# A decoder layer on one core: the second norm's chain with an up unit split ahead of it, turns placed inside products, and one head's turn moved up by a product

## The chip, the cores and the metric

The kernel runs on one core of a Trainium2 chip. The metric is the device time of one execution in microseconds (us); before the change the median of three runs is 770.14 us (770.01 to 772.16). Lower is better. In the profile PE is the matrix engine, PEld its weight load (which runs beside a product), DVE the vector engine, ACT the scalar engine, POOL the GpSimd engine, and SP and ACTq are queues that issue DMA transfers.

## The reference, cut to what matters

One decoder layer for 512 tokens of width 1024. The part around the change is the end of the mixer and the start of the feed-forward block:

```python
mix = jnp.concatenate([h, y], axis=-1) @ w_out[l]        # 512 x 2048 times 2048 x 1024
x = x + g1 * rms_norm(mix, mix_post_g[l])                # first residual (x1 in the kernel)
u = rms_norm(x, ffn_pre_g[l]) * (1.0 + sc2) + sh2        # second norm
up = causal_dwconv(u @ ffn_up[l], ffn_conv_w[l], ffn_conv_b[l])   # 1024 -> 2 x 2816, then 3 taps over tokens
a, gt = jnp.split(up, 2, axis=-1)
f = (jax.nn.silu(gt) * a) @ ffn_down[l]
```

`h` comes from four attention-like heads, `y` from a convolution branch. Before them stand a first norm and the input projection; after them the down projection and a last norm.

## The kernel before

Every weight product is made of three matmuls: an operand is split into a high part (`h` at the end of a name, a copy on ACT) and a low part (`l`, the difference, on DVE or POOL), and `mm3` issues high x high, high x low and low x high. A weight of 1 MB is loaded by one DMA into one of two `raws` buffers and split in four pieces, so a load waits until the last split of the load two before it is done.

The places the change touches, in order of time:

- **Heads.** For each head, `attention(h)` is a generator; its last step turns the head's result (`hn`) on PE into two banks (`hT`), and ACT and DVE split it into `hh` and `hl`. `make_vo(h + 1)` is a generator with one 24-matmul product (`vo`) per token tile of 128. After the third head (h = 2) the turn stands behind the fourth `vo` product, and right ahead of a column sum (`ry_s`) and the next head's scores (`s`), which use the same two `at` banks as the turn.
- **The output projection's second half** (`mixb`, four tiles of 128 tokens). The first 8 blocks of the contraction are done for all tiles together; the last 8 (`mix_last`, 24 matmuls a tile) go tile by tile, so that the second norm of a tile can run while later tiles are still multiplied.
- **The chain of a tile.** `chain_sums` (square sum of `mixb` on ACT, the product `un` with the gain row on DVE, a factor `rm` that POOL raises to -1/2), `chain_x` (the new residual `x1` in two halves, their square sums on ACT, the product `un` with the row `gs2r`, a factor `rf`), `chain_u` (two halves of `un` with factor and row `sh2r`), `turn_tile` (eight 128x128 turns on PE into two banks `xT`), `turn_out` (ACT writes `u2h`, DVE writes `u2l`).
- **The up units.** `w_up` has 22 units of 1 MB; a unit gives two banks (`a` and gate). The first `NE` units are multiplied on token halves of 256 (`up_half`), since the first half of the tokens is ready before the second; the others on all 512.

Inside `with in_order()` ACT, DVE and POOL keep the order in which the code is written. PE and SP keep the written order everywhere. Outside it a scheduler orders ACT, DVE and POOL. PSUM has four `mm` banks, two `at` banks and two `cv` banks. `mixb` of tiles 0 and 1 sits in the `at` banks, of tiles 2 and 3 in the `cv` banks, and `turn_tile` takes `at` banks, so the turn of tile 0 needs the banks of `mixb` 0 and 1.

Of the kernel before, what the change touches and what calls it, by code (L numbers as in the profile page):

```python
# [13 lines left out]
AF = mybir.ActivationFunctionType  # L14
ALU = mybir.AluOpType
# [40 lines left out]
def decoder_layer(ctx, tc, w_glu0, x, c, adaT, vecs, w_glu, w_qko, w_v0, w_vo, w_out, w_up, w_down, out):  # L56
# [664 lines left out]
    def token_factor(sq, name):  # L721

        t = small.tile([P, 1], F32, tag="tt", name=f"{name}t")
        last_factor[0] = V.tensor_scalar(out=t, in0=sq[:, :1], scalar1=sq[:, 1:2], scalar2=D * EPS, op0=ALU.add, op1=ALU.add)
        r = small.tile([P, 1], F32, tag="tr", name=f"{name}r")
        G.tensor_tensor(out=r, in0=t, in1=mhalf[:, :1], op=ALU.pow)
        return r
# [115 lines left out]
    for h in range(H - 1):  # L843
        head_load(h + 1)
        steps = attention(h)
        if h == 0:
            head_proj(1, 0)
            next(steps)
            head_proj(1, 1)
            pace()  # L850
            next(steps)
            pace()
            head_proj(1, 2)
            pace()
            next(steps)
        else:
            next(steps)
            head_proj(h + 1, 0)
            pace()
            for _ in turns:  # L860
                pass
            head_proj(h + 1, 1)
            pace()
            next(steps)
            scaled = last_e[0]
            pace()
# [12 lines left out]
        if h == 0:  # L879
            next(steps)  # L880
            pace()
        make_E(h + 1)
        if h == H - 2:
            norm_mean()
        next(values)
        next(values)
        if h < H - 2:
            turns = steps
        else:
            for _ in steps:  # L890
                pass
        if h == H - 2:
            norm_sums()

# [51 lines left out]
        for tt, ps in enumerate(banks):  # L946
            mm3(ps, (hy[k][0][:, tok(tt)], hy[k][1][:, tok(tt)]), wo[n_ % 4], n_ == 0, False)
    V.scalar_tensor_tensor(out=gains[:, KT : 2 * KT], in0=sc2[:, :, 0], scalar=1.0, in1=vcols("ffn_pre_g", 0, KT), op0=ALU.add, op1=ALU.mult)
    S.activation(gains[:, 2 * KT : 3 * KT], sc2[:, :, 1], AF.Copy)
    S.activation(gains[:, KT : 2 * KT], gains[:, KT : 2 * KT], AF.Copy, scale=RD)  # L950
    wo = [w for g in range(KA // 4, 4) for w in wo_rows(1, g)]
    for tt in range(NT):
        for hf in range(2):
# [8 lines left out]
    def chain_sums(tt):  # L962

        ps = banks[tt]
        sq_sum(ps, msq[:, 2 * tt + 1 : 2 * tt + 2], f"mixb{tt}")
        un = adas.tile([P, D], F32, tag="ada", name=f"un{tt}")
        uns[tt] = [un[:, :T], un[:, T:]]
        V.tensor_tensor(out=uns[tt][1], in0=ps, in1=g1r[1], op=ALU.mult)
        return token_factor(msq[:, 2 * tt : 2 * tt + 2], f"rm{tt}")

    def chain_x(tt, r):

# [11 lines left out]

    turned = {}

    def turn_tile(tt):
        turned[tt] = [atbank(f"xT{tt}_{hf}") for hf in range(2)]
        for tp, un in zip(turned[tt], uns[tt]):
            for i in range(NT):  # L990
                PE.transpose(tp[:, i * P : (i + 1) * P], un[:, i * P : (i + 1) * P], ident)
# [21 lines left out]
        q = len(up_w[i])  # L1013
        up_w[i].append(w_split(r[:, q * T : (q + 1) * T], f"wup{i}_{q * T}", pool, tag, V))

    NE = 3
    early = []

    def up_half(th, i, only=None):
        for half, ps in enumerate(early[i]):  # L1020
# [3 lines left out]
                mm3(ps[:, th * HT : (th + 1) * HT], blk(up_w[i], half * KT + k), (u2h[:, th, k, :], u2l[:, th, k, :]), k == 0, k == KT - 1)  # L1024

    up_w = {0: w_load(w_up[0], "wup0", slots, "t", V)}
    send_rows(KT, 2 * KT, nc.sync)
    gs2r = row(1, cvtile, "gs2", nc.sync)
    sh2r = row(2, cvtile, "sh2", nc.sync)
    raw1 = raw_up(1)  # L1030
    raw2 = raw_up(2)
    early += [[mmbank(f"up{i}_{half}") for half in range(2)] for i in range(2)]
    with in_order():
        for tt in range(3):
            mix_last(tt, 0, 2 * KT - KA)
        r = chain_sums(0)
        r = chain_x(0, r)
        up_split(1, raw1, slots, "t")
        chain_u(0, r)
        turn_tile(0)  # L1040
        mix_last(3, 0, 7)
        r = chain_sums(1)
        up_split(1, raw1, slots, "t")
        r = chain_x(1, r)
        up_split(1, raw1, slots, "t")
        chain_u(1, r)
        turn_out(0)
        turn_tile(1)
        mix_last(3, 7, 2 * KT - KA)
        r = chain_sums(2)  # L1050
        turn_out(1)
        r = chain_x(2, r)
        up_split(1, raw1, slots, "t")
        chain_u(2, r)
        up_half(0, 0)
        turn_tile(2)
        r = chain_sums(3)
        up_split(2, raw2, wpool, "w")
        r = chain_x(3, r)
        up_split(2, raw2, wpool, "w")  # L1060
        chain_u(3, r)
        up_half(0, 1)
        up_split(2, raw2, wpool, "w")
        early.append([cvbank(f"up2_{half}") for half in range(2)])
        up_half(0, 2, 0)
        turn_tile(3)
        turn_out(2)
        up_split(2, raw2, wpool, "w")
        turn_out(3)
    up_half(0, 2, 1)  # L1070
    for i in range(NE):
        up_half(1, i)
    for tt in range(NT):
        for hf in range(2):
            nc.scalar.dma_start(x1_d[tt][hf], x1[tt][hf])


    def halves(z):
        return z.rearrange("p (h t) -> p h t", h=2)

    def conv3(ps, i, name):
        t = cvtile(f"{name}c")
# [44 lines left out]
    for i in range(NF):  # L1127
        if i < NE:
            pa, pg = early[i]
        else:  # L1130
            pieces = w_load(w_up[i], f"wup{i}")
# [240 lines left out]
```

## Time and profile before

| | |
|---|---|
| runs | 772.16, 770.01, 770.14 us; median 770.14 |
| profiled execution | 771.9 us, of which the span of the trace is 770.2 and 1.7 lie around it |
| granted PE clock | 0.998 of full |
| busy in the span | PE 758.1 us (98%), PEld 629.9 (82%), DVE 575.3 (75%), POOL 522.8 (68%), ACT 407.4 (53%) |
| where the change acts | 296 to 316 us (third head) and 385 to 452 us (second norm, units 0 to 2) |

A start time is counted from the start of the span. In a timeline row the columns are start, length (for merged rows, of all of them), engine, line and operation with output and inputs, and in brackets the idle time before it and what ended that. A PE row's length includes a pipelined end, so the distance between two starts is what a matmul costs.

### The profile page before, as it was taken

Reading aid. Unit: us, or ns where it says so; the run is one execution under the profiler, and the core shown is the slowest. Engines: PE = TensorE matmul, PEld = TensorE weight load, DVE = VectorE, ACT = ScalarE, POOL = GpSimd, SP = SyncE. Lnnn points to the kernel's source line nnn. Section 1 sums busy time; section 2 is a strip of 40 time slices with the busy share of each in tenths; the row PEclk is TensorE's granted clock in tenths of the full one; section 3 lists DMA queues with packets and bytes.
Section 4 is the critical chain, followed back from the end, with each engine's and each line's share of the span. In section 5 each row is a group of like instructions: output and inputs, shape, how many; then the busy total and the mean of one; then the engine's idle time right before and its main releaser. Section 6 shows DMA issues by size and latency. Waiting matters only on the chain.

```text
span 770.2 us, 10269 instructions
## 1 busy us (share of the span) xinstructions
PE 758.1 (98%) x3552; PEld 629.9 (82%) x3552; DVE 575.3 (75%) x831; ACT 407.4 (53%) x780; POOL 522.8 (68%) x432
## 2 busy tenths in 40 slices
PE   8999999999999999999998999999999999999996
PEld 6888898878788788788887998888888888888885
DVE  6769999979889686577949798665776578754548
ACT  6685538585665555563334554434444345566633
POOL 4789849794594871645521467876988786699934
PEclk9999999999999999999999999999999999999999
DMA  8973214311131350656953655756586683896273
GB/s 315 365 266 134 86 56 149 125 55 55 55 114 52 110 212 8 246 191 200 371 188 108 251 181 207 283 214 240 193 300 222 224 296 145 316 398 243 95 235 148
DMA packets 40138, 147.34 MB, mean 191 GB/s; under 512 B 3827, under 2 KB 5267, under 8 KB 30485
## 3 DMA queue, kind: packets, MB, share of 16 engines
q1 hardware_dynamic: 26372, 94.50, 34.2%
q10 hardware_dynamic: 13712, 52.18, 18.8%
q8 instruction: 28, 0.46, 0.2%
q14 instruction: 26, 0.20, 0.1%
HBM read 126.59 MB, written 20.07 MB: 190 GB/s over the span
## 4 chain that ended last, share of the span: by engine, by line
PE 88%; DMA 5%; DVE 2%; issue 2%; POOL 1%; ACT 1%; SPq 0%; DVEq 0%; POOLq 0%; ACTq 0%
PE up L210 31%; PE qko L210 13%; PE dn L210 10%; PE vo L210 9%; PE glu L210 7%; PE mixa L210 6%; PE glu L350 4%; PE s L551 2%; PE o L562 2%; DMA wup<-in_w_up 2%; PE v L210 1%; DMA p<-spill_t 1%; PE mixb L210 1%; DMA wglu<-in_w_glu 1%; DMA xn<-in_x 1%
## 5 line engine op out<-in xcount | busy, mean ns | idle before, releaser
L774 DVE SCALAR_TENSOR_TENSOR cv<-gt,cvw,cv 128x485 f32<-128x485 f32 (+24 forms) x200 | 137.1, 730 | 2.1 <-ACT cv L762 0.8
L770 POOL TENSOR_TENSOR cs<-cs,cs 128x510 f32<-128x510 f32 (+3 forms) x32 | 42.1, 1316 | 0.4 <-ACT cs L768 0.3
L210 PE MATMUL up<-u2h,wup_0h 128*128 128x512 f32 (+1 forms) x100 | 36.5, 365 | 0.0
L210 PE MATMUL up<-u2l,wup_0h 128*128 128x512 f32 (+1 forms) x100 | 36.5, 365 | 0.0
L210 PE MATMUL up<-u2h,wup_1024h 128*128 128x512 f32 (+1 forms) x100 | 36.4, 364 | 0.0
L210 PE MATMUL up<-u2h,wup_0l 128*128 128x512 f32 (+1 forms) x100 | 36.4, 364 | 0.0
L210 PE MATMUL up<-u2h,wup_1536l 128*128 128x512 f32 (+1 forms) x100 | 36.4, 364 | 0.0
L210 PE MATMUL up<-u2h,wup_512h 128*128 128x512 f32 (+1 forms) x100 | 36.4, 364 | 0.0
L210 PE MATMUL up<-u2l,wup_512h 128*128 128x512 f32 (+1 forms) x100 | 36.4, 364 | 0.0
L210 PE MATMUL up<-u2h,wup_512l 128*128 128x512 f32 (+1 forms) x100 | 36.4, 364 | 0.0
L210 PE MATMUL up<-u2h,wup_1536h 128*128 128x512 f32 (+1 forms) x100 | 36.4, 364 | 0.0
L210 PE MATMUL up<-u2l,wup_1536h 128*128 128x512 f32 (+1 forms) x100 | 36.4, 364 | 0.0
L210 PE MATMUL up<-u2h,wup_1024l 128*128 128x512 f32 (+1 forms) x100 | 36.4, 364 | 0.0
L210 PE MATMUL up<-u2l,wup_1024h 128*128 128x512 f32 (+1 forms) x100 | 36.3, 363 | 0.0
L176 DVE SCALAR_TENSOR_TENSOR junk<-ada,cb 128x1024 bf16<-128x1024 f32 x20 | 31.8, 1588 | 5.5 <-DMA ada<-in_adaT 5.3
L192 POOL TENSOR_TENSOR wup_0l<-wup,wup_0h 128x512 fp32r<-128x512 f32 x19 | 29.3, 1542 | 4.5 <-ACT wup_0h L191 4.5
L192 POOL TENSOR_TENSOR wup_1024l<-wup,wup_1024h 128x512 fp32r<-128x512 f32 x19 | 25.0, 1318 | 9.4 <-ACT wup_1024h L191 9.4
L192 POOL TENSOR_TENSOR wup_1536l<-wup,wup_1536h 128x512 fp32r<-128x512 f32 x19 | 27.2, 1430 | 4.8 <-ACT wup_1536h L191 4.5
L768 ACT ACTIVATE cs<-gt,cvw 128x511 f32<-128x511 f32 (+4 forms) x40 | 27.1, 713 | 6.0 <-POOL cs L770 3.5
L1105 POOL TENSOR_TENSOR b<-b 128x512 f32<-128x512 f32 x11 | 14.6, 1331 | 18.6 <-PE up L210 10.6
L1106 DVE TENSOR_TENSOR b<-b 128x512 f32<-128x512 f32 x11 | 19.4, 1761 | 10.1 <-POOL b L1105 10.1
L192 POOL TENSOR_TENSOR wup_512l<-wup,wup_512h 128x512 fp32r<-128x512 f32 x19 | 25.2, 1324 | 0.0
(1097 smaller groups left out, 2730.8 us busy)
## 6 DMA issues: line engine op xcount, KB each, us to landing
wup<-in_w_up SPq DMA_DIRECT2D x22, 1024.0 KB, 6.0
b<-in_w_down ACTq DMA_DIRECT2D x11, 1024.0 KB, 5.5
spill_t<-b ACTq DMA_DIRECT2D x11, 1024.0 KB, 4.2
ada<-in_adaT ACTq DMA_DIRECT2D x20, 512.0 KB, 4.2
wqko<-in_w_qko SPq DMA_DIRECT2D x9, 1024.0 KB, 4.8
ada<-in_adaT SPq DMA_DIRECT2D x16, 512.0 KB, 7.0
wo<-in_w_out SPq DMA_DIRECT2D x8, 1024.0 KB, 4.8
wvo<-in_w_vo SPq DMA_DIRECT2D x6, 1024.0 KB, 4.7
```

What stands on the lines that cost most here:

```text
L176: t = V.scalar_tensor_tensor(out=junk, in0=r, scalar=1.0, in1=cb, op0=ALU.mult, op1=ALU.mult, accum_out=mod[:, i : i + 1])
L192: (eng or G).tensor_tensor(out=lo[:, :n], in0=src, in1=hi[:, :n].bitcast(F32), op=ALU.subtract)
L210: PE.matmul(ps, l, r, start=start and i == 0, stop=stop and i == 2, skip_group_check=again)
L350: PE.matmul(ps, blk(wk, i)[a], u[k][b], start=k == 0 and p == 0, stop=k == KT - 1 and p == 1)
L551: PE.matmul(sp[:, :n], ks[d][:, cc * P : (cc + 1) * P], qs[d][:, cc * P :], start=d == 0, stop=d == 1)
L562: PE.matmul(o[:, : DH + 2], E[h][cc][:, a : a + P], vs[h][cc], start=cc == 0, stop=cc == tt)
L768: S.activation(t[:, d:], cvx[j][:, : T - d], AF.Copy, scale=w(CK - 1 - d))
L770: G.tensor_tensor(out=side[:, d:], in0=side[:, d:], in1=t[:, d:], op=ALU.add)
L774: tap = V.scalar_tensor_tensor(out=cp[:, d:], in0=cvx[j][:, : T - d], scalar=w(CK - 1 - d), in1=cp[:, d:], op0=ALU.mult, op1=ALU.add)
L1105: G.tensor_tensor(out=b12, in0=b22, in1=b12, op=ALU.subtract)
L1106: V.tensor_tensor(out=b22, in0=b22, in1=b11, op=ALU.subtract)
```

## The change

It does seven things.

1. `next(values)` for the fourth `vo` product moves behind the rest of `attention(h)`, which for h = 2 puts the turn of the third head ahead of that product; for the other heads nothing moves.
2. Two small copies that made the gains of the second norm move from ACT to DVE.
3. `raw_up(1)`, the load of up unit 1, moves ahead of the rows `gs2` and `sh2` on the SP queue, and its four splits go ahead of the first chain instead of between the steps of the chains. The loads of units 2 and 3 are issued between the chains, and their splits come after the last `turn_out` instead of inside the chains.
4. In `chain_sums` the factor is asked for ahead of the product `un`.
5. The turns stand inside the next tile's products (after 3 and 2 of its 8 blocks) or between halves of unit 0. Tile 0 turns into `mm` banks, tile 3 into `cv` banks.
6. `NE` is 2: units 0 and the first bank of unit 1 are multiplied on token halves, the second bank of unit 1 and all of unit 2 on 512 tokens.
7. The stores of `x1` (256 KB each) move from the ACT queue at the end to the SP queue, behind each chain's `chain_x`.

```diff
@@ heads
         next(values)
-        next(values)
         if h < H - 2:
             turns = steps
         else:
             for _ in steps:
                 pass
+        next(values)
@@ gains
-    S.activation(gains[:, 2 * KT : 3 * KT], sc2[:, :, 1], AF.Copy)
-    S.activation(gains[:, KT : 2 * KT], gains[:, KT : 2 * KT], AF.Copy, scale=RD)
+    V.tensor_copy(gains[:, 2 * KT : 3 * KT], sc2[:, :, 1])
+    V.tensor_scalar(out=gains[:, KT : 2 * KT], in0=gains[:, KT : 2 * KT], scalar1=RD, scalar2=None, op0=ALU.mult)
@@ chain_sums
+        r = token_factor(msq[:, 2 * tt : 2 * tt + 2], f"rm{tt}")
         V.tensor_tensor(out=uns[tt][1], in0=ps, in1=g1r[1], op=ALU.mult)
-        return token_factor(msq[:, 2 * tt : 2 * tt + 2], f"rm{tt}")
+        return r
@@ turn_tile
-    def turn_tile(tt):
-        turned[tt] = [atbank(f"xT{tt}_{hf}") for hf in range(2)]
+    def turn_tile(tt, bank=atbank):
+        turned[tt] = [bank(f"xT{tt}_{hf}") for hf in range(2)]
@@ second norm
-    NE = 3
+    NE = 2
+    def x1_store(tt):
+        for hf in range(2):
+            nc.sync.dma_start(x1_d[tt][hf], x1[tt][hf])
     up_w = {0: w_load(w_up[0], "wup0", slots, "t", V)}
+    raw1 = raw_up(1)
     send_rows(KT, 2 * KT, nc.sync)
     gs2r = row(1, cvtile, "gs2", nc.sync)
     sh2r = row(2, cvtile, "sh2", nc.sync)
-    raw1 = raw_up(1)
-    raw2 = raw_up(2)
     with in_order():
-        for tt in range(3):
-            mix_last(tt, 0, 2 * KT - KA)
+        for tt in range(2):
+            mix_last(tt, 0, LAST)
+        for _ in range(4):
+            up_split(1, raw1, slots, "t")
         r = chain_sums(0)
         r = chain_x(0, r)
-        up_split(1, raw1, slots, "t")
+        x1_store(0)
+        raw2 = raw_up(2)
         chain_u(0, r)
-        turn_tile(0)
-        mix_last(3, 0, 7)
+        mix_last(2, 0, 3)
+        turn_tile(0, mmbank)
+        mix_last(2, 3, LAST)
         r = chain_sums(1)
-        up_split(1, raw1, slots, "t")
         r = chain_x(1, r)
-        up_split(1, raw1, slots, "t")
+        x1_store(1)
+        turn_out(0)
         chain_u(1, r)
-        turn_out(0)
+        mix_last(3, 0, 2)
         turn_tile(1)
-        mix_last(3, 7, 2 * KT - KA)
+        mix_last(3, 2, LAST)
         r = chain_sums(2)
+        r = chain_x(2, r)
+        x1_store(2)
+        raw3 = raw_up(3)
         turn_out(1)
-        r = chain_x(2, r)
-        up_split(1, raw1, slots, "t")
         chain_u(2, r)
-        up_half(0, 0)
+        up_half(0, 0, 0)
         turn_tile(2)
+        up_half(0, 0, 1)
         r = chain_sums(3)
-        up_split(2, raw2, wpool, "w")
         r = chain_x(3, r)
-        up_split(2, raw2, wpool, "w")
+        x1_store(3)
         chain_u(3, r)
...
         turn_out(2)
-        up_split(2, raw2, wpool, "w")
+        turn_tile(3, cvbank)
         turn_out(3)
-    up_half(0, 2, 1)
-    for i in range(NE):
-        up_half(1, i)
+        up_half(0, 1, 0)
+        for _ in range(4):
+            up_split(2, raw2, wpool, "w")
+    up_half(1, 0)
+    up_half(1, 1, 0)
+    for k in range(KT):
+        mm3(halves(early[1][1]), blk(up_w[1], KT + k), (u2h[:, :, k, :], u2l[:, :, k, :]), k == 0, k == KT - 1)
+    for _ in range(4):
+        up_split(3, raw3, wpool, "w")
```

How the instructions then stand, at three places. On SP, behind the load of up unit 0 (`wup0`) in the second norm, this stood before (`row_d` are the two rows on their way through memory, `gs2r` and `sh2r` the rows as they come back, `x1d` the stored residual):

```order
L199 DMA wup0_3754<-in_w_up 128x2048
L696 DMA row_d1_1416<-gTs8_3774 8x128
L696 DMA row_d2_1417<-gTs8_3774 8x128
L702 DMA gs2r0_3778<-row_d1_1416 128x512
L702 DMA gs2r1_3779<-row_d1_1416 128x512
L702 DMA sh2r0_3782<-row_d2_1417 128x512
L702 DMA sh2r1_3783<-row_d2_1417 128x512
L1008 DMA wup1_3786<-in_w_up 128x2048
L1008 DMA wup2_3788<-in_w_up 128x2048
```

and this stands there now:

```order
L199 DMA wup0_3754<-in_w_up 128x2048
L1009 DMA wup1_3772<-in_w_up 128x2048
L696 DMA row_d1_1416<-gTs8_3776 8x128
L696 DMA row_d2_1417<-gTs8_3776 8x128
L702 DMA gs2r0_3780<-row_d1_1416 128x512
L702 DMA gs2r1_3781<-row_d1_1416 128x512
L702 DMA sh2r0_3784<-row_d2_1417 128x512
L702 DMA sh2r1_3785<-row_d2_1417 128x512
L1025 DMA x1d0_0_1419<-x1_0_3552 128x512
L1025 DMA x1d0_1_1420<-x1_0_3552 128x512
L1009 DMA wup2_3875<-in_w_up 128x2048
```

The load of unit 1 has moved ahead of the rows, and the load of unit 2 behind the first stores of the residual.

On DVE, at the first chain (`gTs8` is the turned gains on their way to `row_d`), before:

```order
L192 TENSOR_TENSOR wup0_1536l_3769<-wup0_3754,wup0_1536h_3768 128x512
L694 COPY gTs8_3774<-gT8_3772 16x128
L968 TENSOR_TENSOR un0_3868<-mixb0_3569,g1r_3554 128x512
L724 TENSOR_SCALAR rm0t_3870<-msq_1427 128x1
L975 SCALAR_TENSOR_TENSOR x1_0_3552<-mg0_3548,rm0r_3872,x1_0_3552 128x512
L975 SCALAR_TENSOR_TENSOR x1_0_3552<-un0_3868,rm0r_3872,x1_0_3552 128x512
L978 TENSOR_TENSOR un0_3868<-x1_0_3552,gs2r0_3778 128x512
L978 TENSOR_TENSOR un0_3868<-x1_0_3552,gs2r1_3779 128x512
L724 TENSOR_SCALAR rf0t_3883<-xsq0_3874 128x1
L192 TENSOR_TENSOR wup1_0l_3888<-wup1_3786,wup1_0h_3887 128x512
L983 SCALAR_TENSOR_TENSOR un0_3868<-un0_3868,rf0r_3885,sh2r0_3782 128x512
```

and after, where the four low splits of unit 1 stand ahead of the chain and none inside it:

```order
L694 COPY gTs8_3776<-gT8_3774 16x128
L192 TENSOR_TENSOR wup1_0l_3837<-wup1_3772,wup1_0h_3836 128x512
L192 TENSOR_TENSOR wup1_512l_3841<-wup1_3772,wup1_512h_3840 128x512
L192 TENSOR_TENSOR wup1_1024l_3845<-wup1_3772,wup1_1024h_3844 128x512
L192 TENSOR_TENSOR wup1_1536l_3849<-wup1_3772,wup1_1536h_3848 128x512
L724 TENSOR_SCALAR rm0t_3855<-msq_1427 128x1
L969 TENSOR_TENSOR un0_3854<-mixb0_3569,g1r_3554 128x512
L976 SCALAR_TENSOR_TENSOR x1_0_3552<-mg0_3548,rm0r_3857,x1_0_3552 128x512
```

On PE, between the products of tiles 2 and 3, before:

```order
L210 MATMUL mixb2_3571<-wo1_3_1536h_3740,yl7_3269 128x512
L991 MATMUL xT0_0_3893<-ident_93,un0_3868 128x128 x4
L991 MATMUL xT0_1_3894<-ident_93,un0_3868 128x128 x4
L210 MATMUL mixb3_3572<-wo1_2_0h_3710,yh2_3154 128x512
L210 MATMUL mixb3_3572<-wo1_2_0l_3711,yh2_3154 128x512
```

and after, where tile 0 has been turned 15 matmuls earlier and tile 1 stands six matmuls into tile 3:

```order
L210 MATMUL mixb2_3571<-wo1_3_1536h_3740,yl7_3269 128x512
L210 MATMUL mixb3_3572<-wo1_2_0h_3710,yh2_3154 128x512
L210 MATMUL mixb3_3572<-wo1_2_0l_3711,yh2_3154 128x512
L210 MATMUL mixb3_3572<-wo1_2_0h_3710,yl2_3155 128x512
L210 MATMUL mixb3_3572<-wo1_2_512h_3714,yh3_3160 128x512
L210 MATMUL mixb3_3572<-wo1_2_512l_3715,yh3_3160 128x512
L210 MATMUL mixb3_3572<-wo1_2_512h_3714,yl3_3161 128x512
L992 MATMUL xT1_0_3948<-ident_93,un1_3915 128x128 x4
L992 MATMUL xT1_1_3949<-ident_93,un1_3915 128x128 x4
L210 MATMUL mixb3_3572<-wo1_2_1024h_3718,yh4_3250 128x512
```

More of the change, by code (lines that the diff above doesn't have):

```diff
@@ L1014, in up_split, with halves @@
         up_w[i].append(w_split(r[:, q * T : (q + 1) * T], f"wup{i}_{q * T}", pool, tag, V))
-    NE = 3
+    NE = 2
     early = []
+    def halves(z):
+        return z.rearrange("p (h t) -> p h t", h=2)
+    def x1_store(tt):
+        for hf in range(2):
+            nc.sync.dma_start(x1_d[tt][hf], x1[tt][hf])
     def up_half(th, i, only=None):
@@ L1029, in decoder_layer @@
     sh2r = row(2, cvtile, "sh2", nc.sync)
-    raw1 = raw_up(1)
-    raw2 = raw_up(2)
-    early += [[mmbank(f"up{i}_{half}") for half in range(2)] for i in range(2)]
+    LAST = 2 * KT - KA
     with in_order():
-        for tt in range(3):
-            mix_last(tt, 0, 2 * KT - KA)
+        for tt in range(2):
+            mix_last(tt, 0, LAST)
+        for _ in range(4):
+            up_split(1, raw1, slots, "t")
         r = chain_sums(0)
         r = chain_x(0, r)
-        up_split(1, raw1, slots, "t")
+        x1_store(0)
+        raw2 = raw_up(2)
@@ L1051, in decoder_layer @@
+        x1_store(2)
+        raw3 = raw_up(3)
         turn_out(1)
-        r = chain_x(2, r)
-        up_split(1, raw1, slots, "t")
         chain_u(2, r)
-        up_half(0, 0)
+        early += [[mmbank(f"up{i}_{half}") for half in range(2)] for i in range(NE)]
+        up_half(0, 0, 0)
         turn_tile(2)
+        up_half(0, 0, 1)
         r = chain_sums(3)
-        up_split(2, raw2, wpool, "w")
         r = chain_x(3, r)
-        up_split(2, raw2, wpool, "w")
+        x1_store(3)
         chain_u(3, r)
-        up_half(0, 1)
@@ L1063, in decoder_layer @@
-        up_split(2, raw2, wpool, "w")
-        early.append([cvbank(f"up2_{half}") for half in range(2)])
-        up_half(0, 2, 0)
-        turn_tile(3)
         turn_out(2)
-        up_split(2, raw2, wpool, "w")
+        turn_tile(3, cvbank)
         turn_out(3)
-    up_half(0, 2, 1)
-    for i in range(NE):
-        up_half(1, i)
[L1073 to L1079, printed above, removed]
+        up_half(0, 1, 0)
@@ L1130, in decoder_layer @@
         else:
-            pieces = w_load(w_up[i], f"wup{i}")
+            pieces = up_w.get(i) or w_load(w_up[i], f"wup{i}")
             if i in AT:
```

## The prediction

> **What bounds the kernel now.** I read the page first, then who waits for whom on PE, then PE's rows in order of time where it waits.
>
> ```profile
> PE 758.1 (98%) x3552; PEld 629.9 (82%) x3552; DVE 575.3 (75%) x831; ACT 407.4 (53%) x780; POOL 522.8 (68%) x432
> ```
> ```profile
> PE xT L991 <- DVE u2l L999: 1.4, 1, 1.4
> PE xT L991 <- DVE un L968: 0.6, 1, 0.6
> ```
>
> PE is busy for 98% of the span, so only two things shorten it: fewer or cheaper matmuls, and fewer of PE's own waits. These two of its few waits lie where this change acts (engine and line that waits, what it waited for, total, times, longest). The rows around the turns show what they cost with their edges (the distance between two starts is a matmul's price):
>
> ```profile
> 405.29 0.39 PE L210 MATMUL mixb<-wo_1536h,yl 128*128 128x512 f32 x1
> 405.52 0.60 PE L991 MATMUL xT<-ident,un 128*128 128x128 f32 x4
> 406.69 0.66 PE L991 MATMUL xT<-ident,un 128*128 128x128 f32 x4 [0.57 <-DVE un L968]
> 407.10 0.48 PE L210 MATMUL mixb<-wo_0h,yh 128*128 128x512 f32 x1
> 407.42 0.40 PE L210 MATMUL mixb<-wo_0l,yh 128*128 128x512 f32 x1
> ...
> 411.73 0.39 PE L210 MATMUL mixb<-wo_1024h,yl 128*128 128x512 f32 x1
> 413.55 1.26 PE L991 MATMUL xT<-ident,un 128*128 128x128 f32 x8 [1.43 <-DVE u2l L999]
> 414.56 0.47 PE L210 MATMUL mixb<-wo_1536h,yh 128*128 128x512 f32 x1
> ...
> 415.34 0.28 PE L210 MATMUL up<-u2h,wup_0h 128*128 128x256 f32 x1
> 415.62 0.39 PE L210 MATMUL up<-u2l,wup_0h 128*128 128x256 f32 x1
> 415.84 0.28 PE L210 MATMUL up<-u2h,wup_0l 128*128 128x256 f32 x1
> ...
> 421.36 1.04 PE L991 MATMUL xT<-ident,un 128*128 128x128 f32 x8
> 422.15 0.36 PE L210 MATMUL up<-u2h,wup_0h 128*128 128x256 f32 x1
> ```
>
> From 407.42 to 411.73 lie 19 steps of a 512-wide matmul: 0.2268 us each. An undisturbed turn takes 422.15 - 421.36 = 0.79. Between the products of tiles 2 and 3, 407.10 - (405.29 + 0.23) = 1.58 pass, 0.79 too much; between 411.73 and 414.56 it is 2.83 - 0.23 - 0.79 = 1.81 too much; and 415.34 to 415.84 is two steps of a 256-wide matmul, 0.24, in 0.50: 0.26 too much. Sum of the stalls: **2.86 us**. Why they are there, the rows of the chain say:
>
> ```profile
> 394.89 0.60 ACT L717 ACTIVATE mixb0junk<-mixb 128x512 bf16<-128x512 f32 x1 [6.05 <-PE mixb L210]
> 403.35 0.63 ACT L191 ACTIVATE wup_0h<-wup 128x512 fp32r<-128x512 f32 x1 [3.71 <-DMA wup<-in_w_up]
> ```
> ```profile
> 395.61 0.69 DVE L968 TENSOR_TENSOR un<-mixb,g1r 128x512 f32<-128x512 f32 x1 [4.49 <-ACT mixb0junk L717]
> 396.22 0.20 DVE L724 TENSOR_SCALAR rm0t<-msq 128x1 f32<-128x1 f32 x1
> 397.08 0.75 DVE L975 SCALAR_TENSOR_TENSOR x<-mg,rm0r,x 128x512 f32<-128x512 f32 x1 [0.66 <-POOL rm0r L726]
> ...
> 398.42 1.29 DVE L978 TENSOR_TENSOR un<-x,gs2r 128x512 f32<-128x512 f32 x2
> 399.67 0.21 DVE L724 TENSOR_SCALAR rf0t<-xsq 128x1 f32<-128x1 f32 x1
> 404.01 0.69 DVE L192 TENSOR_TENSOR wup_0l<-wup,wup_0h 128x512 fp32r<-128x512 f32 x1 [4.13 <-ACT wup_0h L191]
> 404.62 1.41 DVE L983 SCALAR_TENSOR_TENSOR un<-un,rf0r,sh2r 128x512 f32<-128x512 f32 x2
> ```
>
> DVE sat idle for 4.13 us inside tile 0's chain, since the split that the code put there waited for a load. Tile 0 was thus 4 us late, and all later tiles behind it on DVE.
>
> **The change part by part.** *Splits ahead of the chain, turns inside products (edits 3 to 5).* Without the split, tile 0's chain runs from 394.89 to rf0t at 399.67, POOL's power (0.86, as from rm0t at 396.22 to x at 397.08), and the last `un` pair, 1.41: 401.9. With the factor asked for ahead of `un`, the 0.61 of `un` (395.61 to 396.22) moves under the power: 401.3. PE ends tile 1's product at 407.10 less 1.58 less 24 x 0.2268 = 400.07, does nine matmuls of tile 2 (2.04) and wants tile 0 at 402.1: 0.8 us to spare. I carried all four chains on with the spacings of these rows. A tile takes DVE 0.61 for the first `un`, 0.1 for rm, 1.34 for `x` (397.08 to 398.42), 1.25 for the next `un` pair, 0.2 for rf, 1.4 for the last pair and some 1.25 for the two halves of `u2l`, 6.1 in all with about 0.3 of waits, against 24 x 0.2268 + 0.8 = 6.2 on PE. On this sheet the halves of tile 1 are there 0.6 before PE wants them, those of tile 2 almost 2, of tile 3 0.4 to 0.7. No turn waits any more for the `at` banks of `mixb`. So all 2.86 go, provided that the splits ahead don't push the first chain. That hangs on the load of unit 1:
>
> ```profile
> 387.43 1.75 POOL L192 TENSOR_TENSOR wo_1536l<-wo,wo_1536h 128x512 fp32r<-128x512 f32 x1
> ```
> ```profile
> 385.16 0.21 ACT L949 ACTIVATE gains<-mod 128x8 f32<-128x8 f32 x1 [6.34 <-DVE mod L181]
> ```
> ```profile
> 392.44 0.82 SPq L702 DMA_DIRECT2D gs2r<-row_d  x2
> 394.30 0.86 SPq L1008 DMA_DIRECT2D wup<-in_w_up  x2
> ```
> ```profile
> 386.00:388.00 2.00, 2.00 (x11) 1.65 (x10) 0.69 (x2) 1.98 (x5) 1.82 (x2) 1.00 0.00 0
> DMA to landing us min/median/max: 4.7/4.8/10.6
> ```
>
> The load needs the buffer of the last output weight, whose last split ended at 387.43 + 1.75 = 389.2. That split waited behind two small copies which held ACT for 6.34 us; they move to DVE (0.2 us there, ahead of nothing that waits), so POOL can follow its splits without the gap: I put its end, and the issue, at 387.5 (earliest 386.7, latest 389.2 as before). The DMA engines are idle then (share 0.00 in the window row). The last row is that of the 1 MB loads of `w_load`: 4.7 to 10.6 us from issue to landing, median 4.8, so it lands at 392.3. DVE's first split starts 0.66 after ACT's (403.35 and 404.01) and four take 4 x 0.61 (404.01 to 404.62): done at 395.4, while the first chain is due on DVE at 395.6. By my sheet no PE wait appears until the load lands at 392.8, and beyond that PE loses one for one. I take **0.2 us** for it; ends 0 and 7.0 (389.2 + 10.6 - 392.8).
>
> The row stores and `gs2r` stand behind this load on SP now; `row_d` follows the turned gains as before, the rows follow at about 392.5 as in 392.44 above, and have no two loads behind them: nothing. The stores of `x1` hold SP until each `chain_x`; the loads behind them (units 2, 3) are needed by PE over 20 us later: nothing, and ACT is rid of eight issues.
>
> Does POOL's power stretch under `un`?
>
> ```profile
> 406.83 0.91 POOL L726 TENSOR_TENSOR rm1r<-rm1t,mhalf 128x1 f32<-128x1 f32 x1 [6.32 <-DVE rm1t L724]
> 414.89 0.54 POOL L726 TENSOR_TENSOR rm2r<-rm2t,mhalf 128x1 f32<-128x1 f32 x1 [3.69 <-DVE rm2t L724]
> ```
>
> It took 0.91 under a weight split and 0.54 under `u2l`, which reads a PSUM bank as `un` does. I take 0.54; the other end costs 0.37 a tile, which the 0.4 to 0.8 to spare cover.
>
> *Fewer token halves (edit 6).* Half of the 288 narrow matmuls (144) become 72 wide ones.
>
> ```profile
> 434.60 0.28 PE L210 MATMUL up<-u2h,wup_0h 128*128 128x256 f32 x1
> 440.36 0.28 PE L210 MATMUL up<-u2h,wup_0h 128*128 128x256 f32 x1
> ```
> ```profile
> 416.00:418.00 2.00, 2.00 (x19) 2.00 (x18) 2.00 (x4) 0.83 (x3) 0.00 (x0) 1.00 0.10 38
> ```
>
> A narrow unit half is 48 matmuls in 5.76 us, 0.120 each; a wide one costs 0.2268. 72 x (2 x 0.120 - 0.2268) = **0.95 us** saved. The window (columns: length, PE, PEld) says why: in a narrow stretch the weight load is busy for 2.00 of 2.00 us, against 82% over the whole span. The Trainium skill, TensorE: Matmul & The Clock Gate, section Back-to-back issue gap, gives N/2.4 + 2.5 ns for one matmul alone, by which 72 times 2 x 109.2 - 215.8 ns would save only 0.19 us, as an estimate; the trace's 120 ns disagrees with that formula and fits the section's other sentence, that in a stream weight load and matmul set the spacing together.
>
> *Third head (edit 1).*
>
> ```profile
> 312.87 1.12 PE L551 MATMUL s<-q_0c,k_2c 128*128 128x512 f32 x2 [0.45 <-DVE hl L600]
> ```
>
> The scores waited 0.45 us for a bank that the split of the turned head still held; with a product of 24 x 0.2268 = 5.4 us between, it is free. One more switch between turns and products costs about 0.1 (407.10 to 407.42 is 0.32 for a step of 0.23): **0.35 us** saved; ends 0 and 0.45.
>
> *Splits of units 2 and 3 on DVE after the last turn.* Eight of 0.61 stand ahead of the convolution of unit 0, whose bank unit 2 now takes. By the same sheet PE wants it at 437.4 and DVE frees it at about 435: nothing, unless DVE waits for a modulation weight as it did here:
>
> ```profile
> 438.62 1.39 DVE L176 SCALAR_TENSOR_TENSOR junk<-ada,cb 128x1024 bf16<-128x1024 f32 x1 [3.42 <-DMA ada<-in_adaT]
> ```
>
> With 3.42 once, the cover of 2.4 is gone and PE waits 1.0.
>
> Sum: -2.86 - 0.95 - 0.35 + 0.2 = -4.0 us. Against the profiled execution, 771.9, this is 767.9; the median stands 1.8 below that execution, and I predict against it: 770.14 - 4.0 = **766.1 us**. From unit 2 on PE waits for nothing that the list shows, so what is won there should stay won.
>
> **Rivals.** (a) The load lands late: issued at 389.2 and landing after 4.8 to 6, at 394.0 to 395.2, it costs 1.2 to 2.4 instead of 0.2: 767.1 to 768.3. For it: in this trace it took from 394.30 to 403.35 with another load beside it; against: nothing is beside it now. (b) The same mechanism far enough to lose: from a landing at 396.8 on all 4.0 are spent, and at 389.2 + 10.6 = 399.8 the time is 770.14 - 4.2 + 7.0 = 773. This is the slower side. (c) The rows come late. If the row store must wait for the load ahead of it on its queue (392.3) and then takes its 1.3 (391.15 before, gs2r at 392.44), the rows are issued at 393.6; landing in 4.9 they come at 398.5, where the chain wants them at 397.7: 0.8, of which PE's reserve covers part: 766.1 to 766.9.
>
> ```profile
> 391.15 0.64 SPq L696 DMA_DIRECT2D row_d<-gTs  x2
> DMA to landing us min/median/max: 4.0/4.9/6.9
> ```
>
> The Trainium skill, DMA: Bandwidth & Descriptors, section Queues, rings and completion order, has each DMA engine take a queue's descriptors in ring order, which speaks for (c); no row before shows a small store behind a load. (d) Unit 2 waits for its bank, above: 1.0, so 767.1, at the outside 2: 768.1. (e) It does not do what it says: PE reaches unit 2 earlier and waits later by as much for splits, 770. Against it: the list of PE's waits has none after the turns.
>
> **How the numbers follow.** Forecast (at most 0.5 of stalls left) 0.55; (a) 0.20, half of it still more than 0.3% (2.3 us, about what a measurement of this kernel tells from no change) faster; (b) 0.06; (c) 0.07; (d) 0.07, 0.04 of it faster; (e) 0.05. Faster 0.55 + 0.10 + 0.07 + 0.04 = 0.76; same 0.10 + 0.03 + 0.05 = 0.18; slower 0.06. The range goes from all terms at their best with a little for the run-to-run spread, 764.9, to the middle of (e) and past all of (a), (c) and (d), 769.2; it leaves out (b), half of (e) and a few hundredths below.
>
> **What the profile after would show.** No PE wait above 0.3 at `xT`, none at `s`; the load of unit 1 issued near 387.5 with ACT's first split of it near 392.3, and mixb0's square sum at 394.9; 0.227 per step in unit 2; unit 2 ends near 448.3 where it ended at 440.36 + 2 x 5.76 = 451.9. Wrong would be: DVE idle ahead of unit 1's splits beyond 393, a wait of `up` for DVE at the start of unit 2, or a new wait in later units.

## The result, and the profile after

The changed kernel takes 768.39 us (767.29 to 769.16); the kernel before, timed beside it, 770.34 us. The ratio is 0.9966, with a 95% interval of 0.9955 to 0.9976: faster by 0.34%, or 2.6 us (1.8 to 3.5). The forecast was 766.1 us, 4.0 below 770.14, the median of before that it started from. The sign was right; of the forecast 4.0 us the medians show 1.95 and the ratio 2.6.

The profiled execution took 769.16 us (span 767.4), that of before 771.9 (span 770.2). First the head of the page and the list of who waits for whom on PE (engine and line that waits, what it waited for, total, times, longest), both of the changed kernel:

```profile
span 767.4 us, 10129 instructions
...
PE 756.0 (99%) x3480; PEld 625.1 (81%) x3480; DVE 576.6 (75%) x837; ACT 410.7 (54%) x778; POOL 516.5 (67%) x428
```
```profile
PE cps L159 <- ACT crow L158: 2.9, 1, 2.9
PE glu L350 <- ACT uh L371: 1.3, 1, 1.3
PE glu L350 <- ACT uh L405: 0.9, 1, 0.9
```

The waits at `xT` and at `s` are gone; what is left lies in the first 50 us, where nothing was changed. The turns and the load of unit 1 in the timeline of the changed kernel:

```profile
403.20 1.03 PE L992 MATMUL xT<-ident,un 128*128 128x128 f32 x8
408.87 1.03 PE L992 MATMUL xT<-ident,un 128*128 128x128 f32 x8
416.71 1.04 PE L992 MATMUL xT<-ident,un 128*128 128x128 f32 x8
420.45 1.04 PE L992 MATMUL xT<-ident,un 128*128 128x128 f32 x8
```
```profile
393.58 0.63 ACT L191 ACTIVATE wup_0h<-wup 128x512 fp32r<-128x512 f32 x1 [3.85 <-DMA wup<-in_w_up]
```
```profile
388.68 0.33 SPq L1009 DMA_DIRECT2D wup<-in_w_up  x1
391.30 0.64 SPq L696 DMA_DIRECT2D row_d<-gTs  x2
393.82 0.82 SPq L702 DMA_DIRECT2D gs2r<-row_d  x2
```

Each turn is one piece of eight with no wait in brackets. Where the time went is read from marks, starts of the same PE instruction in both traces: first product of the input projection (`qko`), first `mixa`, first `mixb`, first `up`, unit 3, end.

| us between marks | before | after | difference |
|---|---|---|---|
| start to first qko | 115.25 | 116.94 | +1.69 |
| qko to mixa (third head) | 200.44 | 199.85 | -0.59 |
| mixa to mixb | 51.59 | 51.58 | 0.0 |
| mixb to first up (turns of tiles 0, 1) | 48.06 | 45.47 | -2.59 |
| first up to unit 3 (turns 2, 3; units 0 to 2) | 36.54 | 35.34 | -1.20 |
| unit 3 to the end | 318.3 | 318.3 | 0.0 |

Behind the first qko these two executions differ by 4.4 us, but 1.7 of it is lost in an opening whose instructions are the same in both. So two questions were open: does the change slow the opening, and is the 2.59 at the turns what every execution of before pays?

### The profile page after: what moved, and what is told of

Read it like the earlier page. It is cut to its first block, busy times and chain, and to the rows that moved or that the text cites. A ratio compares the mean times of both kernels' runs of the same rounds, so it can differ in the third digit from the quotient of the medians.

```text
span 767.4 us, 10129 instructions
## 1 busy us (share of the span) xinstructions
PE 756.0 (99%) x3480; PEld 625.1 (81%) x3480; DVE 576.6 (75%) x837; ACT 410.7 (54%) x778; POOL 516.5 (67%) x428
## 4 chain that ended last, share of the span: by engine, by line
PE 93%; DMA 4%; POOL 1%; ACT 1%; issue 0%; DVEq 0%; SPq 0%; DVE 0%; POOLq 0%; ACTq 0%
PE up L210 31%; PE dn L210 13%; PE qko L210 13%; PE vo L210 9%; PE glu L210 7%; PE mixa L210 6%; PE mixb L210 6%; DMA wglu<-in_w_glu 3%; PE o L562 2%; PE s L551 2%; PE v L210 2%; PE glu L350 1%; DMA xn<-in_x 1%; PE xT L992 0%; PE hT L593 0%
## 5 line engine op out<-in xcount | busy, mean ns | idle before, releaser
L192 POOL TENSOR_TENSOR wup_0l<-wup,wup_0h 128x512 fp32r<-128x512 f32 x18 | 25.0, 1389 | 19.4 <-ACT wup_0h L191 19.3
L176 DVE SCALAR_TENSOR_TENSOR junk<-ada,cb 128x1024 bf16<-128x1024 f32 x20 | 29.9, 1493 | 2.6 <-DMA ada<-in_adaT 2.5
L192 POOL TENSOR_TENSOR wup_1536l<-wup,wup_1536h 128x512 fp32r<-128x512 f32 x18 | 24.6, 1365 | 6.0 <-ACT wup_1536h L191 5.4
L191 ACT ACTIVATE wup_512h<-wup 128x512 fp32r<-128x512 f32 x22 | 13.8, 629 | 25.7 <-PE up L210 20.9
L330 DVE SCALAR_TENSOR_TENSOR junk<-ada,cps 128x1024 bf16<-128x1024 f32 x16 | 19.5, 1220 | 9.8 <-DMA ada<-in_adaT 9.2
```

Of the source, the lines that this page charges most:

```text
L176: t = V.scalar_tensor_tensor(out=junk, in0=r, scalar=1.0, in1=cb, op0=ALU.mult, op1=ALU.mult, accum_out=mod[:, i : i + 1])
L191: S.activation(hi[:, :n], src, AF.Copy)
L192: (eng or G).tensor_tensor(out=lo[:, :n], in0=src, in1=hi[:, :n].bitcast(F32), op=ALU.subtract)
L330: V.scalar_tensor_tensor(out=junk, in0=first[k][:, i * D : (i + 1) * D], scalar=1.0, in1=cps, op0=ALU.mult, op1=ALU.mult, accum_out=part[: ...
```

## The experiments

The theories: A, the opening differs by chance and unit 1's load was slowed by unit 2's beside it; B, the change slows the opening; C, the edits are worth less than their marks; D, E and F, further causes of the late load and of the stall, are stated where they came up. Ratios are to the kernel before in runs on the same chip; its median there was 771.4 to 771.6.

**Repeats of both kernels.** No edit.

> The kernel before, unchanged, once more. Its trace is wanted for its marks. In the two traces so far the first product of the input projection (qko) starts at 115.2 us before and at 116.9 after the change, although the instructions up to there are the same. Theory A (the opening, bound by its loads, differs from one execution to the next): this trace shows its qko mark anywhere from 114.5 to 117.5, and total minus mark keeps 655.0 +- 0.4 of the span. Theory B (the change makes the opening slower every time): the mark stays at 115.2 +- 0.4. Both: ratio 1.000 +- 0.001.

> The changed kernel, unchanged, once more. Theory A: the qko mark lies anywhere from 114.5 to 117.5, the span behind the mark is 650.5 +- 0.4, and the time is -4.4 against before plus whatever its opening does by chance, over many executions -4. Theory B (opening slower each time): mark 116.9 +- 0.4 again, ratio near 0.9965 (-2.7). Theory C (the edits are worth half of what the traces say): the span behind the mark is over 652.

Measured: before again 0.9998 (0.9989 to 1.0007); after again 0.9966 (0.9954 to 0.9978), 768.77 us. The qko marks are 116.61 and 116.17, so this time before has the later opening. In the repeat of before PE's list has no `xT` at all:

```profile
PE cps L159 <- ACT crow L158: 2.9, 1, 2.9
PE glu L350 <- ACT uh L371: 2.0, 1, 2.0
PE s L551 <- DVE hl L600: 0.5, 1, 0.5
PE up L210 <- DVE u2l L999: 0.2, 1, 0.2
```

B's mark of 115.2 for before is refuted, and what I had taken as a property of the kernel, the stalls at the turns, is not in every execution. Behind the qko mark before took 653.0 here against 654.9, outside the +-0.4 that A allowed; after took 650.5 both times.

**Parts.** In the first kernel the order of the fourth product and the turn alone is changed (edit 1); the second has all but that.

```diff
-        next(values)          # head_only: before, with the product behind the turn
         if h < H - 2:
             turns = steps
         else:
             for _ in steps:
                 pass
+        next(values)
```

> Before, with only the third head's turn moved ahead of the fourth product (edit 1). By the marks of the two traces it is worth 0.6 us between the first product of qko and the first of mixa, where 0.35 was predicted: ratio 0.9992 (0.9988 to 0.9996). Theory B would put the slower opening in one of the edits; if it is in this one, the mark is at 116.9 and the ratio 1.0014. Theory A: the mark is free, and the ratio 0.9992.

> After, with the third head's turn back behind the fourth product (edits 2 to 7 without edit 1). By the marks the second norm is worth 3.8 us: ratio 0.9951 if the opening is like that of before, 0.9973 if the slower opening (1.7) belongs to these edits (theory B), and 0.9975 or more if the gain in the norm is less than the marks say (theory C).

Measured: 0.9996 (0.9986 to 1.0006) and 0.9968 (0.9955 to 0.9981). Times alone can't tell 0.6 us here; marks can. From qko to mixa pass 199.85 to 199.87 in the six traces that have edit 1 and 200.44 to 200.46 in those that don't: edit 1 is worth 0.59 and nothing else touches this stretch. The qko marks are 116.43 and 116.01: the later opening comes with neither part.

**Why the load is late.** Two edits on before, one load each:

```diff
-    raw2 = raw_up(2)          # u2_later: written behind chain_x(1) instead
...
-    raw1 = raw_up(1)          # u2_first: unit 2's load ahead of unit 1's
-    raw2 = raw_up(2)
+    raw2 = raw_up(2)
+    raw1 = raw_up(1)
```

> Before, with one edit: the load of up unit 2 is issued behind tile 1's chain_x instead of right behind unit 1's load. In the three traces of kernels with the old second norm, unit 1's load landed 9.05, 7.1 and 8.0 us after its issue, with unit 2's load beside it, and PE stood 2.60, 0 and 0.37 us at the turns. Theory A (unit 1's load is slowed by unit 2's beside it, by a different amount in each execution, and PE's stall at the turns is what of that is not covered): it lands 4.7 to 5.5 after its issue, no PE wait at xT, second norm from first mixb to first up at 45.5, and the time is about 1.0 below before (the mean of 2.60, 0 and 0.37): ratio 0.9987 (0.9980 to 0.9995). Theory D (the load is slow for another reason): it lands after 7 to 9 us again and the ratio is 1.000.

> Before, with the loads of units 1 and 2 issued in the other order, so that unit 1's is the later of two. Theory A with queue order (a DMA engine works off the first load first): unit 2 lands after about 5, unit 1 about 9.5 after the first issue, later than in any trace so far (about 404 us), and PE stands 2.6 to 3.5 at the turns: ratio 1.002 to 1.0035. If the two loads share the engines evenly, unit 1 lands after 7 to 9 as before and the ratio is 1.000 (0.999 to 1.001). Theory C (stalls at the turns do not set the time): ratio 1.000 with the longer stalls in the trace.

Measured: 0.9995 (0.9983 to 1.0006) and 1.0061 (1.0047 to 1.0075). The first, SP and then ACT in its timeline:

```profile
393.13 0.82 SPq L702 DMA_DIRECT2D gs2r<-row_d  x2
394.04 0.85 SPq L702 DMA_DIRECT2D sh2r<-row_d  x2
394.99 0.86 SPq L1008 DMA_DIRECT2D wup<-in_w_up  x2
```
```profile
402.80 0.63 ACT L191 ACTIVATE wup_0h<-wup 128x512 fp32r<-128x512 f32 x1 [1.46 <-DMA wup<-in_w_up]
```

The edit of u2_later did not do what its text says. The last SP row still holds two loads (x2), as in before: between the old place and the new one the code gives SP nothing to issue and nothing to wait for, so unit 2's load follows unit 1's at once. Unit 1's took 402.80 - 394.99 = 7.81 us, inside what before shows, and the run decides nothing between A and D. What stands ahead of unit 1's load on the queue are the four row loads, 128x512 each, together 1 MB. With unit 2's load ahead as well (u2_first) it starts to be split at 406.69 and PE waits at three places:

```profile
PE xT L991 <- DVE un L983: 2.2, 1, 2.2
PE xT L991 <- DVE u2l L999: 1.4, 1, 1.4
...
PE xT L991 <- DVE un L968: 0.6, 1, 0.6
```

4.2 us of waits, and 1.0061 is 4.7 us: stalls at the turns do set the time, against C. They were more than either version of A expected: with one more load ahead on the queue, unit 1's split starts 2.5 to 5.4 us later behind the first mixb than in the six traces with the old order (third column of the table below).

**The same in the changed kernel.** `raw_up(1)` is put back behind the rows, all else as after.

```diff
-    raw1 = raw_up(1)
     send_rows(KT, 2 * KT, nc.sync)
     gs2r = row(1, cvtile, "gs2", nc.sync)
     sh2r = row(2, cvtile, "sh2", nc.sync)
+    raw1 = raw_up(1)
```

> After, with unit 1's load issued behind the rows gs2 and sh2 again, as before the change, while its four splits stay ahead of the first chain. Issue near 394.3 instead of 388.7 (by before's order), landing 4.7 to 5.5 later, 399.0 to 399.8. In the after trace the splits start at the landing (393.58), un of tile 0 is done 8.8 later (402.4), and the turn came at 403.20. So PE should stand 399.0 + 8.8 - 403.2 = 4.6 to 5.4 us at the first xT, and the time be that much above after: ratio to before 1.0026 to 1.0037. A rival: tile 0's delay is partly taken up behind (tiles 1 to 3 have reserves of 0.6 to 2 us): PE still loses the first wait, so no less than 4.6. If the load lands late without a PE wait, the one-for-one rule of the prediction is wrong.

Measured: 1.0076 (1.0059 to 1.0092), slower than before, and a wait of 5.8 us where 4.6 to 5.4 was expected. SP and ACT:

```profile
393.14 0.38 SPq L1009 DMA_DIRECT2D wup<-in_w_up  x1
```
```profile
400.23 0.63 ACT L191 ACTIVATE wup_0h<-wup 128x512 fp32r<-128x512 f32 x1 [11.76 <-DMA wup<-in_w_up]
```

The load was split 7.09 us after its issue, with only the rows ahead of it and nothing beside it: the next load was issued at 405.99. In the five traces that have the new norm with the load ahead of the rows it took 4.7 to 5.0. So the rows alone make the load 2 us late, and theory A's cause, unit 2's load beside it, isn't needed for that. Then, in the timeline and in windows of 2 us (columns: length, busy of PE, PEld, DVE, ACT and POOL, granted clock, DMA share, GB/s):

```profile
402.23 0.39 PE L210 MATMUL mixb<-wo_1024h,yl 128*128 128x512 f32 x1
408.39 1.97 PE L992 MATMUL xT<-ident,un 128*128 128x128 f32 x8 [5.77 <-DVE un L984]
410.01 0.78 PE L210 MATMUL mixb<-wo_1536h,yh 128*128 128x512 f32 x1
410.59 0.63 PE L210 MATMUL mixb<-wo_1536l,yh 128*128 128x512 f32 x1
...
411.75 0.39 PE L210 MATMUL mixb<-wo_0l,hh 128*128 128x512 f32 x1
411.99 0.39 PE L210 MATMUL mixb<-wo_0h,hl 128*128 128x512 f32 x1
```
```profile
402.00:404.00 2.00, 0.62 (x3) 0.19 (x1) 2.00 (x5) 0.99 (x3) 0.40 (x1) 1.00 0.00 0
404.00:406.00 2.00, 0.00 (x0) 0.00 (x0) 1.94 (x4) 0.94 (x3) 0.14 (x1) 0.70 0.10 40
406.00:408.00 2.00, 0.00 (x0) 0.00 (x0) 1.34 (x4) 1.19 (x4) 0.55 (x1) 0.50 0.96 308
408.00:410.00 2.00, 1.61 (x8) 1.61 (x9) 1.95 (x5) 0.00 (x0) 0.54 (x1) 0.50 0.98 397
410.00:412.00 2.00, 2.00 (x8) 1.63 (x7) 2.00 (x4) 1.35 (x4) 0.00 (x0) 0.60 0.42 159
412.00:414.00 2.00, 2.00 (x10) 1.66 (x9) 1.90 (x5) 1.07 (x4) 0.54 (x1) 1.00 0.38 144
```

From first mixb to first up this kernel takes 53.00, 7.53 more than after: 5.94 because the turn starts later, and 1.59 because the clock fell to 0.50 in the idle time and came back only near 411.6, 3.2 us after PE started again. This is rival (b)'s mechanism, with its price higher than the prediction's one for one.

**Unit 1's load ahead of the rows in the old kernel, and two more executions of it.** The first is before with that one line moved (unit 2's load stays behind the rows).

> Before, with one edit: unit 1's load is issued ahead of the rows gs2 and sh2 (unit 2's stays behind them), all else as before. Theory E (unit 1's load is late because the 1 MB of rows stands ahead of it on its queue, not because of unit 2's load beside it): issue near 389.2, landing 4.9 later near 394.1, DVE's split of unit 1 no longer waits for a DMA, no PE wait at xT, whatever the opening. Theory A (unit 2's load beside it): the same here, but it has u2_later against it. Time: what the stalls at the turns cost before on average, 0.4 to 1.0 us: ratio 0.9987 to 0.9995. If they cost 2.6 in most executions, as the prediction took it, 0.9966.

> The kernel before again, for one more pair of opening and stall. Theory F (the load of unit 1 does not move with PE's opening, so a late opening uses up the stall at the turns): with the first qko at 116.0 or later the turns cost under 0.6 us together; only an early opening near 115.3 shows 2 us or more. If the stall has nothing to do with the opening, an opening after 116 can have a stall of 2 us.

> The kernel before once more, for the same purpose: with the first qko at 116.0 or later the stalls at the turns are under 0.6 us by theory F; the span behind the first qko is 652.6 to 653.4 then, and near 655 with an opening at 115.3.

Measured: 0.9984 (0.9975 to 0.9994) for the one line, with no wait at `xT` and 45.47 from mixb to first up, as in after: as theory E has it. Theory A expected the same here; what speaks against A is u1_behind_rows, and not u2_later. The two executions of before had openings of 116.29 and 115.33, and against theory F it is the later one that stalled (0.8 us at `xT`), while the early one didn't. What decides is seen when the start of unit 1's first split is set against the first mixb. For the execution with the 0.8, PE, ACT and PE again:

```profile
368.34 0.39 PE L210 MATMUL mixb<-wo_0h,hh 128*128 128x512 f32 x1
```
```profile
402.98 0.63 ACT L191 ACTIVATE wup_0h<-wup 128x512 fp32r<-128x512 f32 x1 [2.28 <-DMA wup<-in_w_up]
```
```profile
414.97 0.28 PE L210 MATMUL up<-u2h,wup_0h 128*128 128x256 f32 x1
```

| kernel | first qko | split of unit 1 after first mixb | first mixb to first up | over 45.47 |
|---|---|---|---|---|
| u2_first | 116.08 | 38.56 | 50.55 | 5.08 |
| before | 115.25 | 36.07 | 48.06 | 2.59 |
| rep_before2 | 116.29 | 34.64 | 46.63 | 1.16 |
| head_only | 116.43 | 34.23 | 46.21 | 0.74 |
| u2_later | 116.93 | 33.81 | 45.80 | 0.33 |
| rep_before3 | 115.33 | 33.54 | 45.52 | 0.05 |
| rep_before | 116.61 | 33.16 | 45.48 | 0.01 |

In the first six rows the loss is the third column less 33.48, to 0.02 us: one for one. The old order lives on the edge of this line: its load lands 7.1 to 9.1 us after issue, the four executions of before paid 2.59, 1.16, 0.05 and 0.01, on average 0.95 (0.81 with head_only and u2_later, whose loads stand as in before), and the one move of a load saved 1.2 us (0.5 to 1.9). The one the prediction was worked out from is the worst of the four. With the new order the split starts 23.8 to 25.7 us behind the first mixb (five traces), and mixb to first up takes 45.47 or 45.48 in each.

**Token halves.** After, with the second bank of unit 1 and unit 2 multiplied on halves of 256 tokens again.

```diff
+    up_half(0, 1, 1)
     up_half(1, 0)
-    up_half(1, 1, 0)
-    for k in range(KT):
-        mm3(halves(early[1][1]), blk(up_w[1], KT + k), (u2h[:, :, k, :], u2l[:, :, k, :]), k == 0, k == KT - 1)
+    up_half(1, 1)
...
+                if i == 2:    # unit 2, in the loop over units
+                    for th in range(2):
+                        for k in range(KT):
+                            mm3(ps[:, th * HT : (th + 1) * HT], blk(pieces, half * KT + k), (u2h[:, th, k, :], u2l[:, th, k, :]), k == 0, k == KT - 1)
```

> After, with the second bank of unit 1 and all of unit 2 on token halves again (edit 6 alone undone). By the prediction's term, 72 x (2 x 0.120 - 0.2268), units 1 and 2 take 0.95 us longer and the time is 0.95 above after: ratio to before 0.9978 where after has 0.9966. If the 1.2 us that the marks give between first up and unit 3 were all of this edit, 0.9982. By the Trainium skill, TensorE: Matmul & The Clock Gate, section Back-to-back issue gap, as an estimate, 0.19 us: 0.9969.

Measured: 0.9978 (0.9969 to 0.9987). By the marks, first up to unit 3 takes 36.27 instead of 35.34: 0.93, as the term said (0.95). The formula of the Trainium skill for one matmul alone (TensorE: Matmul & The Clock Gate, section Back-to-back issue gap) gives 0.19, as an estimate: the trace disagrees with it.

**Gains copies on ACT again.** After without edit 2.

```diff
-    V.tensor_copy(gains[:, 2 * KT : 3 * KT], sc2[:, :, 1])
-    V.tensor_scalar(out=gains[:, KT : 2 * KT], in0=gains[:, KT : 2 * KT], scalar1=RD, scalar2=None, op0=ALU.mult)
+    S.activation(gains[:, 2 * KT : 3 * KT], sc2[:, :, 1], AF.Copy)
+    S.activation(gains[:, KT : 2 * KT], gains[:, KT : 2 * KT], AF.Copy, scale=RD)
```

> After, with the two small gains copies back on ACT (edit 2 undone). POOL's last split of the output weight then waits for ACT again, and the load of unit 1 is issued 389.0 to 389.5 (by 389.2 in before's trace) instead of 388.68 as in after. It lands 4.9 later, 393.9 to 394.4. In after a landing at 393.58 left 0.8 us at the first turn, so PE waits 0 to 0.3 there: ratio to before 0.9966 to 0.9970, the span behind the first qko 650.5 to 650.8 (650.5 in both traces of after). If edit 2 were needed for the gain, the wait would be over 1 us.

Measured: 0.9961 (0.9949 to 0.9973), after's value within the intervals, though its opening was the latest of all (qko at 117.38). The load was issued at 389.74 and split at 394.48, no turn is in the list of PE's waits, and mixb to first up took 45.48. First up to unit 3 took 35.54 instead of 35.34: the second half of the fourth turn came 0.2 later. Edit 2 is worth 0.2 us at most here, in one trace, and the times don't show it.

## Why the prediction was right, and where its size was off

The sign and the mechanism were right: no wait at `xT` or `s`, PE at 0.227 per step in unit 2, nothing given back after unit 3. Term by term, forecast against what the runs showed:

| term | forecast | shown |
|---|---|---|
| stalls at the turns | -2.60 (0.79 + 1.81) | -2.59 against the profiled execution, -0.95 against the mean of four |
| token halves | -0.95 | -0.93 |
| stall at the first up and the rest of that stretch | -0.26 | -0.34 (36.61, mean of four, less 35.34, less 0.93) |
| third head | -0.35 | -0.59 |
| late load of unit 1 | +0.2 | 0.0 |
| sum | -4.0 | -2.8; by the ratio -2.6 (-1.8 to -3.5) |

**The step that failed** is "Sum of the stalls: 2.86 us", taken off "the median stands 1.8 below that execution, and I predict against it". The stalls hung on a landing, and one trace shows one landing. That execution was 1.8 us above the median, which should have warned that part of its stalls was its own; its own sum, 771.9 - 4.0 = 767.9, is 0.5 from the measured median, though partly by chance, since the opening of that execution (115.25) is the earliest of fourteen. The other part, that stall's true mean, could not be read from one trace. The stalls were booked 1.65 too high (2.60 for 0.95), and 768.39 still lies in the range, up to 769.2, only because its slower part was held open for rivals that did not come: that is luck.

Smaller steps. The third head gave 0.24 more than forecast: I charged 0.1 for "one more switch between turns and products", and the marks show none beyond the wait of 0.45 to 0.5; what the remaining 0.1 is, no run separates. Unit 1's load was issued at 388.68 and split from 393.58; with the first mixb 1.09 later than in before, that is 387.6 and 392.5 in before's time, as forecast (387.5, 392.3). The two copies took 0.16 and 1.24 us on DVE in the profiled execution and not "0.2 us" together (below), and no PE wait came of it. Unit 2 ended at 449.18, 447.5 with the later opening taken off; the 448.3 of the prediction doesn't fit its own sum, by which it is 451.9 - 4.0 = 447.9. The edge was put too early: in u1_behind_rows a split 32.61 behind the first mixb made the first turn 5.94 late, so PE loses from 26.67 on, which is 393.9 in before's time and not "392.8"; after had 25.21.

The rivals. (a) did not come: the load had nothing ahead of it and took 4.9 us. (b) was shown by u1_behind_rows to be real and near: the row order alone turns the gain into a loss of 0.8%. (c)'s mechanism came true, without a price: the row store issued at 391.30 was followed by `gs2r` at 393.82, 2.5 us later instead of 1.29, 0.24 after the load ahead of it began to be split; in gains_act it was 394.70, 0.22 after 394.48. The Trainium skill, DMA: Bandwidth & Descriptors, section Queues, rings and completion order, has each DMA engine consume a queue's descriptors in ring order; these pairs agree, and so does unit 1's load behind the rows. But the store doesn't always wait for the end of the load ahead, as (c) had it: in the repeat of after `gs2r` was issued 0.24 before the load was split, 1.41 after the store.

```profile
386.67 0.33 SPq L1009 DMA_DIRECT2D wup<-in_w_up  x1
389.98 0.64 SPq L696 DMA_DIRECT2D row_d<-gTs  x2
391.39 0.82 SPq L702 DMA_DIRECT2D gs2r<-row_d  x2
```
```profile
391.63 0.63 ACT L191 ACTIVATE wup_0h<-wup 128x512 fp32r<-128x512 f32 x1 [3.56 <-DMA wup<-in_w_up]
```

I had used this rule for the rows behind the load, and missed the same rule for the load behind the rows: "with another load beside it" named at most a part of the cause. The rows alone explain 7.1 us. Whether unit 2's load, or the stores of `x1` that the old code issues on ACT's queue meanwhile, make the rest of the 7.1 to 9.1 that were seen stays open; no run took away one of them alone. (d) and (e) did not come.

The opening: over fourteen traces the first qko starts between 115.25 and 117.38 us, in kernels with the old norm's code (116.2 on average over eight) as in those with the new one (116.4 over six). A difference of 0.2 with this spread shows nothing; theory B is not supported. In that stretch ACT's wait for its weights differs from one execution to another (total, times, longest; before, then after):

```profile
ACT wglu_0h L191 <- DMA wglu<-in_w_glu: 10.4, 8, 2.2
```
```profile
ACT wglu_0h L191 <- DMA wglu<-in_w_glu: 12.6, 8, 3.4
```

These landings don't explain the mark by themselves: in the repeat of before the same line reads 8.8, 6, 2.1, with the opening 1.36 later. What sets the mark stays open.

## What to carry to other kernels

Before a stall is booked as a gain, ask what it waits for: here a stretch bound by PE (qko to mixa) repeated to 0.02 us, a load's time from issue to landing differed by 2 us between executions of the same kernel, and a stall that follows a landing one for one has to be averaged, not read off. If the profiled execution lies above the median, make the sum against it and book against the median only terms that repeat. And look at what stands ahead of a load on its own queue: here one issue moved ahead of 1 MB of rows was worth 1.2 us (0.5 to 1.9) of the 2.6 of the whole change. Last, see in the trace that an edit moved what it was meant to move: the x2 in u2_later's row says that it did not.

## What the hardware showed that was not expected

**A wait of 5.8 us costs more than itself.** PE's last matmul ended at 402.62 (402.23 + 0.39). The window from 404 to 406 has a mean clock of 0.70, between 1.00 before and 0.50 behind it, so the clock fell near 404.8, 2.2 us into the idle time. It was 0.50 when PE started again at 408.39, where a matmul step took 0.42 us (410.59 to 411.01), and the mean of 0.60 from 410 to 412 puts the return near 411.6. In u2_first an idle time of 2.24 left the clock at 1.00 and the loss was one for one. The Trainium skill, TensorE: Matmul & The Clock Gate, section What's actually happening, gives half rate after an idle window of about 3.4 us and full rate after as much busy time: the return, after 3.2 us, agrees, while the fall came sooner than 3.4 us after the last matmul.

**Small DVE instructions waited for POOL's split to end.** Edit 2 let POOL go on without its wait for ACT, and beside it three tiny instructions on DVE took over a microsecond. Changed kernel, DVE and POOL:

```profile
385.03 1.14 DVE L181 TENSOR_TENSOR mod<-mod,vec 128x16 f32<-128x16 f32 x1
386.20 1.21 DVE L948 SCALAR_TENSOR_TENSOR gains<-mod,vec 128x8 f32<-128x8 f32 x1
387.33 0.16 DVE L949 COPY gains<-mod 128x8 f32<-128x8 f32 x1
387.44 1.24 DVE L950 TENSOR_SCALAR gains<-gains 128x8 f32<-128x8 f32 x1
```
```profile
383.87 2.27 POOL L192 TENSOR_TENSOR wo_512l<-wo,wo_512h 128x512 fp32r<-128x512 f32 x1
386.10 1.28 POOL L192 TENSOR_TENSOR wo_1024l<-wo,wo_1024h 128x512 fp32r<-128x512 f32 x1
387.35 1.30 POOL L192 TENSOR_TENSOR wo_1536l<-wo,wo_1536h 128x512 fp32r<-128x512 f32 x1
```

They end at 386.17, 387.41 and 388.68, where POOL's splits end at 386.14, 387.38 and 388.65, 0.03 earlier each time; in before's trace the first two took 0.18 and 0.17 with POOL waiting, and in the repeat of after the last of the four, behind the end of POOL's last split, took 0.17. The Trainium skill, SBUF — State Buffer, section SBUF: two separate sides, calls the port pair that DVE and GpSimd share an exclusive lock held for a whole instruction; these ends agree with it.
